# Softmax over 512 columns: the first store issued ahead of two exponentials of the second tile

## Chip, cores, metric

One core of one Trainium2 chip. The metric is the device time of one execution in microseconds (us). Before: 162.81 us, the median of three runs (162.79 to 162.98).

## The reference

```python
# x: (16, 1024, 512) float32
x_scaled = x / 0.5
x_max = np.max(x_scaled, axis=-1, keepdims=True)
exp_x = np.exp(x_scaled - x_max)
return (exp_x / np.sum(exp_x, axis=-1, keepdims=True)).astype(np.float32)
```

33.55 MB are read and 33.55 MB written.

## The kernel before

The 16384 rows are eight tiles of 128 partitions by 16 rows of 512 floats, 4.19 MB each. There are six buffers, so the seventh tile needs the buffer of the first, and its load waits for the first tile's store. VectorE takes the maxima, the reciprocals and most of the final multiplication; ScalarE takes the exponentials (one per row, with the sum) and one row in eight of the multiplication, and issues the stores.

```python
G = 16
LOADS = [[(0, 4), (4, G)]] + [WHOLE] * 7
BLOCKS = [[(0, 4), (4, 8), (8, G)]] + [WHOLE] * 6 + [[(0, 8), (8, G)]]
STORES = [WHOLE] * 8
SPLIT, TAIL = 6, 2          # seventh tile: its last two rows come by GpSimd
BUFS = 6
# ... cut
if c == SPLIT and hi == G:
    hi = G - TAIL
    for p0, p1 in ((P - 2, P), (0, P - 2)):
        nc.gpsimd.dma_start(out=xt[p0:p1, hi:G, :], in_=xr[c][p0:p1, hi:G, :], max_dma_last_dim=4 * D)
nc.sync.dma_start(out=xt[:, lo:hi, :], in_=xr[c][:, lo:hi, :])
# ... cut: shift (maxima, VectorE), exponentials (ScalarE)
def scale_vector(i):
    k = b - b // 8          # the rows that VectorE multiplies
    # ... cut: reciprocal, tensor_mul of k rows
def scale_scalar(i):
    for g in range(b - b // 8, b):      # the others, on ScalarE
        # ... cut
# ... cut
shift(0)
shift(1)
exponentials(0)
for i in range(n):          # n = 11 blocks; the first tile is blocks 0 to 2
    if i + 1 < n:
        exponentials(i + 1)
    scale_vector(i)
    scale_scalar(i)
    if i + 2 < n:
        shift(i + 2)
    store(i)                # issues on ScalarE's queue when a tile is complete
```

Of the kernel before, what the change touches and what calls it, by code (L numbers as in the profile page):

```python
# [1 line left out]

# [4 lines left out]


@with_exitstack
def kernel(  # L10
    ctx: ExitStack,
    tc: tile.TileContext,
    x: bass.AP,
    out: bass.AP,
):
    nc = tc.nc
    fp32 = mybir.dt.float32
    P = nc.NUM_PARTITIONS
    AX = mybir.AxisListType.X
    EXP = mybir.ActivationFunctionType.Exp  # L20
    COPY = mybir.ActivationFunctionType.Copy
    MAX = mybir.AluOpType.max

    D = x.shape[-1]
    xf = x.flatten_outer_dims()
    of = out.flatten_outer_dims()
    N = xf.shape[0]




    G = 16
    C = N // (P * G)
    assert C * P * G == N
    xr = xf.rearrange("(c p g) d -> c p g d", p=P, g=G)
    outr = of.rearrange("(c p g) d -> c p g d", p=P, g=G)
    WHOLE = [(0, G)]
# [3 lines that stand above are left out]
    SPLIT, TAIL = 6, 2  # L41
    BMAX = 16
    BUFS = 6

    data = ctx.enter_context(tc.tile_pool(name="data", bufs=BUFS))
    stats = ctx.enter_context(tc.tile_pool(name="stats", bufs=6))

    ctx.enter_context(tc.manual_schedule())


    warm = stats.tile([P, 1], fp32, name="warm", bufs=1)
    nc.vector.memset(warm, 0.0)  # L52
    nc.scalar.activation(out=warm, in_=warm, func=EXP)  # L53

    chunks = {}
    blocks = [(c, lo, hi) for c in range(C) for lo, hi in BLOCKS[c]]
    n = len(blocks)
    biases, sums, recips = {}, {}, {}

    def load(c):  # L60
        if c < BUFS:
            chunks[c] = data.tile([P, G, D], fp32, name="xt")
        else:
            chunks[c] = chunks[c - BUFS]
        xt = chunks[c]
        for lo, hi in LOADS[c]:
# [7 lines that stand above are left out]
                    nc.gpsimd.dma_start(  # L74
                        out=xt[p0:p1, hi:G, :],
                        in_=xr[c][p0:p1, hi:G, :],
                        max_dma_last_dim=4 * D,
                    )
            nc.sync.dma_start(out=xt[:, lo:hi, :], in_=xr[c][:, lo:hi, :])  # L79

    def shift(i):
        c, lo, hi = blocks[i]
        if c not in chunks:
            load(c)
        b = hi - lo
        negmax = stats.tile([P, BMAX], fp32, name="negmax")
        nc.vector.tensor_reduce(  # L87
            negmax[:, 0:b], chunks[c][:, lo:hi, :], axis=AX, op=MAX, negate=True
        )
        biases[i] = stats.tile([P, BMAX], fp32, name="bias")  # L90
        nc.vector.tensor_scalar_mul(biases[i][:, 0:b], negmax[:, 0:b], 2.0)  # L91

    def exponentials(i):
        c, lo, hi = blocks[i]
        sums[i] = stats.tile([P, BMAX], fp32, name="sums")
        for g in range(hi - lo):
            row = chunks[c][:, lo + g, :]
            nc.scalar.activation(  # L98
                out=row,
                in_=row,  # L100
                func=EXP,
                bias=biases[i][:, g : g + 1],
                scale=2.0,
                accum_out=sums[i][:, g : g + 1],
            )


    def scale_vector(i):
        c, lo, hi = blocks[i]
        b = hi - lo  # L110
        k = b - b // 8
        recips[i] = stats.tile([P, BMAX], fp32, name="recip")
        nc.vector.reciprocal(recips[i][:, 0:b], sums[i][:, 0:b])  # L113
        rows = chunks[c][:, lo : lo + k, :]
        nc.vector.tensor_mul(  # L115
            rows, rows, recips[i][:, 0:k].unsqueeze(2).broadcast_to((P, k, D))
        )

    def scale_scalar(i):
        c, lo, hi = blocks[i]  # L120
        b = hi - lo
        for g in range(b - b // 8, b):
            row = chunks[c][:, lo + g, :]
            nc.scalar.activation(  # L124
                out=row, in_=row, func=COPY, scale=recips[i][:, g : g + 1]
            )

    def store(i):
        c, _, end = blocks[i]
        for lo, hi in STORES[c]:  # L130
            if hi == end:
                nc.scalar.dma_start(
                    out=outr[c][:, lo:hi, :], in_=chunks[c][:, lo:hi, :]
                )

    shift(0)
    shift(1)
    exponentials(0)
    for i in range(n):
        if i + 1 < n:  # L140
            exponentials(i + 1)
        scale_vector(i)
        scale_scalar(i)
        if i + 2 < n:
            shift(i + 2)
        store(i)


# [1 line left out]
_INS = ['x']  # L150
_OUTS = [((16, 1024, 512), 'float32')]


# [23 lines left out]
```

## Time and profile before

| what | before |
|---|---|
| time | 162.81 us |
| span of the profiled run | 160.9 us |
| VectorE busy, ScalarE busy | 134.6 us (84%), 102.1 us (63%) |
| moved | 67.13 MB, 417 GB/s over the span |
| first store | issued 45.61, landed 71.05 us |
| seventh tile's rows by GpSimd | issued 72.52, landed 103.57 us |
| last store | issued 147.58, landed 159.89 us |

A share of busy time does not tell what sets the end. Here VectorE and DMA both look full. Two lines of the kernel before, the last store's issue (timeline: start, duration, engine, line, operation) and GpSimd's larger piece (list of DMA issues: count, size, us from issue to landing):

```profile
147.58 0.34 ACTq L132 DMA_DIRECT2D out_dram<-xt  x1
```

```profile
xt<-in_x_dram POOLq DMA_DIRECT2D x1, 504.0 KB, 31.1
```

### The profile page before, as it was taken

To read this page: it belongs to the slowest core of one execution; us is meant where nothing else is said; L and a number is where in the kernel's file an instruction comes from. 1 tells how busy PE (TensorE), PEld (TensorE's weight loads), DVE (VectorE), ACT (ScalarE), POOL (GpSimd) and SP (SyncE) were. 2 spreads that over 40 slices of the span, in tenths; PEclk is the share of its full clock that TensorE was granted. 3 is DMA by queue.
4 is the path that set the end of the run, shared out by engine and by line. 5 is a ranking of instruction groups with operands and counts; after the bars stand their busy time and mean duration, and the time that the engine had idled before them with its cause. 6 is when DMAs were issued, how large, how long until landed. Compare 5 with 4: busy or idle time off the path is not lost.

```text
span 160.9 us, 410 instructions
## 1 busy us (share of the span) xinstructions
DVE 134.6 (84%) x45; ACT 102.1 (63%) x273; POOL 1.7 (1%) x6
## 2 busy tenths in 40 slices
DVE  0507999999999999999999999999999999956000
ACT  3071549069979963997299909990999890890000
POOL 0000000000000000012000000000000000000000
DMA  5999999999999999999999999999999999999993
GB/s 175 476 399 505 399 391 513 399 391 507 399 399 375 407 456 440 407 440 441 424 444 417 397 447 462 440 399 464 432 399 464 440 399 456 448 399 440 456 399 138
DMA packets 2642, 67.13 MB, mean 417 GB/s; under 512 B 336, under 2 KB 336, under 8 KB 464
## 3 DMA queue, kind: packets, MB, share of 16 engines
q1 hardware_dynamic: 1296, 33.03, 48.5%
q10 hardware_dynamic: 1152, 33.55, 48.3%
q0 software_dynamic: 192, 0.52, 0.8%
q14 instruction: 2, 0.02, 0.0%
HBM read 33.55 MB, written 33.55 MB: 417 GB/s over the span
## 4 chain that ended last, share of the span: by engine, by line
DVE 79%; DMA 7%; ACT 4%; issue 1%; SPq 0%
DVE negmax L87 42%; DVE xt L115 36%; DMA xt<-in_x_dram 7%; ACT xt L98 4%; DVE bias L91 1%; DVE recip L113 1%; SPq L79 0%
## 5 line engine op out<-in xcount | busy, mean ns | idle before, releaser
L98 ACT ACTIVATE xt<-xt,bias 128x512 f32<-128x512 f32 x128 | 90.4, 708 | 41.7 <-DVE bias L91 41.2
L87 DVE TENSOR_REDUCE negmax<-xt 128x16 f32<-128x8192 f32 (+2 forms) x11 | 69.9, 6352 | 9.5 <-DMA xt<-in_x_dram 9.5
L115 DVE TENSOR_TENSOR xt<-xt,recip 128x7168 f32<-128x7168 f32 (+2 forms) x11 | 62.0, 5637 | 0.4
L98 ACT ACTIVATION_READ_ACCUMULATOR xt<-xt,bias 128x1 f32 x128 | 23.9, 187 | 0.0
L124 ACT ACTIVATE xt<-xt,recip 128x512 f32<-128x512 f32 x15 | 9.9, 707 | 0.0
L113 DVE RECIPROCAL recip<-sums 128x16 f32<-128x16 f32 (+2 forms) x11 | 2.4, 219 | 1.8 <-ACT xt L98 1.8
L91 DVE TENSOR_SCALAR bias<-negmax 128x16 f32<-128x16 f32 (+2 forms) x11 | 1.9, 173 | 0.4
L74 POOL DMA_DIRECT2D xt<-in_x_dram x2 | 1.5, 736 | 71.4 <-DMA out_dram<-xt 71.4
L53 ACT ACT_TABLE_LOAD x1 | 1.3, 1283 | 0.7 <-PEq L161 0.7
L52 DVE MEMSET warm<- 128x1 f32 x1 | 0.1, 59 | 0.8 <-PEq L161 0.8
L53 ACT ACTIVATE warm<-warm 128x1 f32<-128x1 f32 x1 | 0.2, 202 | 0.0
L161 POOL MEMSET const-float32-0.0<- 128x1 f32 x1 | 0.1, 93 | 0.2 <-issue 0.2
L161 POOL MEMSET const-bfloat16-1.0<- 128x1 bf16 x1 | 0.1, 95 | 0.0
L161 POOL MEMSET const-float32-1.0<- 128x1 f32 x1 | 0.1, 93 | 0.0
L161 POOL MEMSET const-uint8-127<- 128x1 uint8 x1 | 0.1, 93 | 0.0
## 6 DMA issues: line engine op xcount, KB each, us to landing
out_dram<-xt ACTq DMA_DIRECT2D x8, 4096.0 KB, 23.7
xt<-in_x_dram SPq DMA_DIRECT2D x6, 4096.0 KB, 35.0
xt<-in_x_dram SPq DMA_DIRECT2D x1, 3584.0 KB, 23.8
xt<-in_x_dram SPq DMA_DIRECT2D x1, 3072.0 KB, 11.7
xt<-in_x_dram SPq DMA_DIRECT2D x1, 1024.0 KB, 4.9
xt<-in_x_dram POOLq DMA_DIRECT2D x1, 504.0 KB, 31.1
xt<-in_x_dram POOLq DMA_DIRECT2D x1, 8.0 KB, 9.3
```

The lines of the kernel that those rows point to most:

```text
L52: nc.vector.memset(warm, 0.0)
L53: nc.scalar.activation(out=warm, in_=warm, func=EXP)
L74: nc.gpsimd.dma_start(out=xt[p0:p1, hi:G, :], in_=xr[c][p0:p1, hi:G, :], max_dma_last_dim=4 * D,)
L87: nc.vector.tensor_reduce(negmax[:, 0:b], chunks[c][:, lo:hi, :], axis=AX, op=MAX, negate=True)
L91: nc.vector.tensor_scalar_mul(biases[i][:, 0:b], negmax[:, 0:b], 2.0)
L98: nc.scalar.activation(out=row, in_=row, func=EXP, bias=biases[i][:, g : g + 1], scale=2.0, accum_out=sums[i][:, g : g + 1],)
L113: nc.vector.reciprocal(recips[i][:, 0:b], sums[i][:, 0:b])
L115: nc.vector.tensor_mul(rows, rows, recips[i][:, 0:k].unsqueeze(2).broadcast_to((P, k, D)))
L124: nc.scalar.activation(out=row, in_=row, func=COPY, scale=recips[i][:, g : g + 1])
L161: nc = _bacc.Bacc("TRN2", target_bir_lowering=False, num_devices=1)
```

## The change

Its intent: the first store is the one whose landing lets the seventh tile load, so it goes out before the last two exponentials of the second tile. The loads, GpSimd's two pieces included, are left as they were.

```diff
-    def exponentials(i):
+    def exponentials(i, rows):
         c, lo, hi = blocks[i]
-        sums[i] = stats.tile([P, BMAX], fp32, name="sums")
-        for g in range(hi - lo):
+        if i not in sums:
+            sums[i] = stats.tile([P, BMAX], fp32, name="sums")
+        for g in rows:
...
-    exponentials(0)
+
+    def rows(i):
+        c, lo, hi = blocks[i]
+        cut = hi - lo - (2 if c == 1 else 0)
+        return range(cut), range(cut, hi - lo)
+
+    exponentials(0, rows(0)[0])
     for i in range(n):
         if i + 1 < n:
-            exponentials(i + 1)
+            exponentials(i + 1, rows(i + 1)[0])
         scale_vector(i)
         scale_scalar(i)
         if i + 2 < n:
             shift(i + 2)
         store(i)
+        if i + 1 < n:
+            exponentials(i + 1, rows(i + 1)[1])
```

## The prediction

> **What bounds the kernel now.** I began with the page of the profile: the slices, then the queues and the issues.
>
> ```profile
> DVE  0507999999999999999999999999999999956000
> ACT  3071549069979963997299909990999890890000
> DMA  5999999999999999999999999999999999999993
> GB/s 175 476 399 505 399 391 513 399 391 507 399 399 375 407 456 440 407 440 441 424 444 417 397 447 462 440 399 464 432 399 464 440 399 456 448 399 440 456 399 138
> HBM read 33.55 MB, written 33.55 MB: 417 GB/s over the span
> out_dram<-xt ACTq DMA_DIRECT2D x8, 4096.0 KB, 23.7
> ```
>
> Two rows are full: VectorE from slice 5 to slice 36, and the DMA from slice 2 to the last but one. So two claims have to be weighed: a chain through VectorE, and the mass of bytes. The chain of waits names VectorE:
>
> ```profile
> DVE 79%; DMA 7%; ACT 4%; issue 1%; SPq 0%
> ...
> 87.42 8.61 DVE negmax L87
> ...
> 96.42 7.19 DVE xt L115
> 103.61 0.35 issue
> 103.96 8.69 DVE negmax L87
> ...
> 137.59 5.76 ACT xt L98 x16
> 143.35 0.02 issue
> 143.37 0.21 DVE recip L113
> 143.59 0.02 issue
> 143.61 3.89 DVE xt L115
> ```
>
> From 12.90 us on this chain has no hole. The 0.35 us "issue" at 103.61 looks like a wait for the seventh tile's load, but the instruction before it, the multiplication that starts at 96.42, takes 7.62 us by the timeline and ends at 104.04; the reduction starts while it drains, as the others do. So VectorE does not wait there, and an earlier load cannot pull it forward. The chain ends in the issue of the last store (timeline, ACT's queue): start 147.58. That store lands at 159.89, and the span ends at 160.9.
>
> Those last 12.3 us are DMA. I went through the records of the single DMA packets in the trace, summed by time. From 2 us to 158 us the packets in flight fill 16.0 of 16 engines in every 2 us, with one dip to 15.8 at 146 to 150 us. A 32 KB packet takes 1.21 us, load or store, and one engine does 8 of them for a whole tile: 9.7 us. The store of the seventh tile ends on 14 of the engines between 148.77 and 149.56 us, on one at 147.52 and on one at 149.87. The early engine begins its part of the last store at about 148.4, some 0.85 us after the issue at 147.58. Thus 14 engines pass from one store to the next without a gap, with only about 148.77 - 148.4 = 0.35 us in hand. **The DMA engines are the bound, from the first load to the last store, and the VectorE chain runs just ahead of them.** The finish is set by the slowest of 16 engines: the final store's completions come at 158.17 to 158.92 on 14 engines, 159.25 on one, 159.55 on the last. The mean over all packets ends near 158.7, so imbalance costs about 0.8 us.
>
> **What the Trainium skill says.** "DMA: Bandwidth & Descriptors", section "Issuing engines are not separate DMA queues": transfers issued from ACT, SyncE and GpSimd run on the same 16 engines and interleave. The trace agrees: when stores join the loads, from 50 us to 112 us, the two queues take about 8 engines each, and the total stays at 16.0. The same page, section "Queues, rings and completion order": each engine alternates between its queues packet by packet. The trace agrees: GpSimd's 504 KB, 4 KB packets of 0.16 us, issue at 72.52 and land only at 103.57, since each of about 9 packets per engine waits its turn behind a 32 KB load packet and a 32 KB store packet. Section "Why a DMA increments its semaphore by 16 and not by 1" says how many engines a transfer uses, and that GpSimd's transfers take consecutive engines from a cursor. Chaining the packets end to start, I find two engines that carry two or three 4 KB packets and 14 that carry seven to ten (the chaining is not perfect: one and nine would fit the shape), so the split into 2 and 126 rows relieves two engines of 8 x 0.16 = 1.3 us. "Perfetto Trace Analysis", section "What "DMA-bound" means", names specific DMA engines as one possible bound; the 159.55 against a median of 158.6 is that case.
>
> **The change, part by part.** Nothing is removed or added: 128 exponentials, 15 scaling rows, 8 stores, the same loads by the same queues, the same VectorE program. One order changes, on ACT, and only in tile two (the condition names it).
>
> ```profile
> 42.76 0.70 ACT L98 ACTIVATE xt<-xt,bias 128x512 f32<-128x512 f32 x1
> ...
> 43.46 0.70 ACT L98 ACTIVATE xt<-xt,bias 128x512 f32<-128x512 f32 x1
> ...
> 44.17 0.70 ACT L98 ACTIVATE xt<-xt,bias 128x512 f32<-128x512 f32 x1
> ...
> 44.87 0.70 ACT L124 ACTIVATE xt<-xt,recip 128x512 f32<-128x512 f32 x1
> 45.61 0.38 ACTq L132 DMA_DIRECT2D out_dram<-xt  x1
> 46.20 0.17 DVE L91 TENSOR_SCALAR bias<-negmax 128x16 f32<-128x16 f32 x1
> 46.28 0.24 DVE L113 RECIPROCAL recip<-sums 128x16 f32<-128x16 f32 x1
> ```
>
> The rows at 43.46 and 44.17 are the fifteenth and sixteenth exponentials of tile two. They move behind the store. The scaling row then starts at 43.46 in place of 44.87, and the store issues at 45.61 - 1.41 = 44.20. Its VectorE input has been ready since 37.6, so nothing else holds it. First gain: **the first store starts 1.4 us sooner**.
>
> What ACT pays: the issue itself. After the issue at 125.53, the next exponential starts at 125.97, so it takes about 0.47 us from the scaling row's end. Before, that stood in an idle gap (ACT waits for a bias until 46.41). After, the two exponentials run at about 44.65 to 46.05, and the read of their sum, which trails by about 0.1 us, ends near 46.15. VectorE's reciprocal needs these sums at 46.28. So it fits, with some 0.1 us in hand; if not, VectorE's chain slips by perhaps 0.1 us, and so does the last store's issue, inside the 0.35 us above.
>
> Downstream: the first store lands at about 69.7 instead of 71.05, which releases the buffer for the seventh tile. SyncE's 14-row load and GpSimd's two pieces go out 1.4 us sooner, and GpSimd's rows land near 102.2 instead of 103.57. Since VectorE gets to them at 103.96 either way, this is margin and not time. The loads of tiles five and six lose a share of DMA in exchange (they landed at 56.43 and 75.80, and are needed at 70.7 and 87.3), harmless.
>
> The sum for the DMA bound: the same 67.1 MB in the same packets on engines that were never idle gives 0. Moving work between the queues of a full resource does not shorten it.
>
> What can move is the imbalance. When the first store joins, about 30 load packets between 47.1 and 50 us take 1.3 to 2.85 us rather than 1.21; the excess sums to some 15 engine-us, 0.9 us per engine. One engine, already about 0.5 us late since an instruction-fetch packet at 37.8, takes the 2.85 us packet: it completes tile five at 56.10 against a median of 54.3, 1.8 us late, and I take it to be the one that finishes last at 159.55, 0.95 us late, after being relieved. An earlier start of the store changes the phase of this event, thus how much the laggard loses. If it loses no more than the others, the end is set by the 159.25 or 158.92 engine: gain 0.3 to 0.6 us. If it loses one more packet's time, the loss is up to 1.2 us. The 2.85 us is the largest of all those packets, so a return towards the usual is likelier than a further rise: I take -0.2 us as my estimate, 162.81 - 0.2 = **162.6 us**.
>
> **The rivals.** (1) The VectorE chain is the true bound and the earlier load shortens it: the 0.35 us at 103.61 would go, 162.45. Against: the multiplication ends at 104.04, so there was no wait. Even then the effect is tiny. (2) The late exponentials hold the reciprocal, and a wait on ACT takes the place of the one removed: up to 0.5 us of slip through a chain without slack, minus the 0.35 us in hand, 162.8 to 163.0. For it: the slack is only 0.1 us. (3) The first store's disturbance meets the loads in a worse phase, and one engine ends later: 163 to 164. For it: one engine did take 1.6 us in one packet. (4) The disturbance vanishes: up to 0.9 us of DMA time saved, but the last store cannot move data before 148.4, so at best 148.4 + 9.7 = 158.1 in place of 159.55: 161.4, which is 0.9%. This is also the floor for every version with this VectorE chain.
>
> **Range and chances.** The floor of 161.4 and a bad phase of one packet (1.2 us, 164.0) bracket what I can imagine; both ends are unlikely. 8 in 10: 162.0 to 163.4. The three times of before span 0.2 us, so noise is small. A 2% step is 3.3 us, more than twice any term above: faster 0.01, within 2% 0.97, slower 0.02.
>
> **What would show it.** Right: the store's issue at about 44.2 in ACT's queue; its landing near 69.7, GpSimd's pieces landing near 102; VectorE's reductions still 16.6 us apart and the last store's issue within 0.15 us of 147.58; DMA slices at 9 throughout. The completions of the last store by engine would tell whether the laggard moved. Wrong: a last store issued over 0.3 us earlier or later (the VectorE chain was moved), a hole in the DMA row, or an end beyond 164 with the issue unmoved, which would mean that one engine fell behind for a reason I have not seen.

## The result, and the profile after

After: 162.66 us, median of four runs (162.54 to 162.85), beside 162.80 us for the kernel before on the same chip. The ratio is 0.9994, 95% interval 0.9976 to 1.0012: the same. (A ratio is the mean time of one kernel's fast runs over that of the other's fast runs of the same rounds, so not quite the ratio of the medians.)

The timeline of the changed kernel where the change is (ScalarE's instructions, and two of VectorE's):

```profile
42.71 0.70 ACT L99 ACTIVATE xt<-xt,bias 128x512 f32<-128x512 f32 x1
...
43.41 0.71 ACT L125 ACTIVATE xt<-xt,recip 128x512 f32<-128x512 f32 x1
44.15 0.38 ACTq L133 DMA_DIRECT2D out_dram<-xt  x1
44.57 0.72 ACT L99 ACTIVATE xt<-xt,bias 128x512 f32<-128x512 f32 x1 [0.45 <-ACT xt L125]
...
45.29 0.71 ACT L99 ACTIVATE xt<-xt,bias 128x512 f32<-128x512 f32 x1
45.90 0.19 ACT L99 ACTIVATION_READ_ACCUMULATOR xt<-xt,bias 128x1 f32 x1
46.15 0.17 DVE L91 TENSOR_SCALAR bias<-negmax 128x16 f32<-128x16 f32 x1
46.24 0.24 DVE L114 RECIPROCAL recip<-sums 128x16 f32<-128x16 f32 x1
```

The store issues at 44.15 in place of 45.61. The two late exponentials start 0.45 us after the scaling row's end (the bracket is ScalarE's idle time), the last sum is read by 46.09, and the reciprocal takes it at 46.24 without a wait.

The same slices, the chain of waits around the seventh tile, the last store, and GpSimd's piece, all of the changed kernel:

```profile
DVE  0607999999999999999999999999999999956000
ACT  3071549069989963998299909990999890790000
POOL 0000000000000000030000000000000000000000
DMA  5999999999999999999999998999999999999993
```

```profile
96.37 2.91 DVE xt L116
99.28 4.64 issue
103.92 8.69 DVE negmax L87
```

```profile
147.53 0.34 ACTq L133 DMA_DIRECT2D out_dram<-xt  x1
```

```profile
xt<-in_x_dram POOLq DMA_DIRECT2D x1, 504.0 KB, 29.6
```

Look at the second of these fences and at its counterpart in the prediction. "4.64 issue" is not a wait that has grown from 0.35 us. The chain steps at 99.28 to the moment at which the load released the reduction, while VectorE was still multiplying until 104.0; both reductions start within 0.04 us of the same time (103.96 and 103.92). So the piece called "issue" is the margin of the load: 0.35 us before, 4.64 us after. The change multiplied this margin, and nothing in this kernel spends it. It is not free: the eighth tile's load landed 0.9 us later than before (115.61, before 114.72), though VectorE reads it only at 120.5. The last store issues at 147.53, 0.05 us from before.

So the time neither went nor came: the first store's issue moved by 1.46 us, its landing by 2.84, GpSimd's rows by 4.33, and the end by about 0.1 us.

To see why, I read the records of the single DMA packets in the trace. A packet of 32 KB takes 1.213 us when nothing disturbs it (28 KB: 1.062, 24 KB: 0.91). "Excess" below is what packets took over that, summed over all that were more than 0.03 us too long, and divided by 16 engines. "Mean end" and "last end" are the mean and the last of the 16 engines' completions of the last store. All times in us, from the one profiled execution of each kernel; the rows below the first two are the experiments.

| kernel | first store issued | last store issued | excess per engine | mean end | last end | time of that run |
|---|---|---|---|---|---|---|
| before | 45.61 | 147.58 | 1.01 | 158.71 | 159.55 | 162.72 |
| after | 44.15 | 147.53 | 1.29 | 159.01 | 159.31 | 162.61 |
| after, again | 44.15 | 147.53 | 1.23 | 158.88 | 159.26 | 162.58 |
| pieces swapped | 44.22 | 147.60 | 1.07 | 158.76 | 159.30 | 162.48 |
| light VectorE | 43.68 | 141.24 | 1.05 | 158.67 | 159.37 | 162.63 |
| before, light VectorE | 44.93 | 141.19 | 1.26 | 158.79 | 159.24 | 162.51 |
| five behind | 41.84 | 147.96 | 1.29 | 158.90 | 159.21 | 162.52 |
| eight behind | 39.76 | 147.72 | 1.68 | 159.25 | 160.26 | 163.44 |
| eight behind, light | 39.49 | 145.86 | 2.18 | 159.79 | 160.70 | 163.95 |
| twelve behind | 37.48 | 148.62 | 1.85 | 159.53 | 159.83 | 163.11 |
| store in halves | 24.82 | 148.23 | 1.40 | 159.12 | 159.58 | 162.82 |
| halves, light | 28.07 | 148.45 | 1.80 | 159.47 | 161.65 | 165.02 |
| store late | 47.88 | 149.68 | 2.01 | 160.35 | 160.67 | 163.87 |
| half a store left out | 44.06 | 147.43 | 1.24 | 158.08 | 158.18 | 161.37 |

Take the excess from the mean end: in the first twelve rows 157.5 to 157.7 remains (the last two, with 158.3 and 156.8, are special: in both, engines stood idle), whether the first store goes out at 25 or at 45 us, and whether the last goes out at 141 or at 149 us. That is the time of 67.13 MB through engines that are never idle. From the last end to the time of the run it is another 3.2 to 3.4 us, always. These twelve can differ from each other only in two small terms: the excess, and how far the last engine lags the mean. This is an account of where the time is, not yet of why. The change moved both, in opposite directions: excess 1.01 to 1.29 (+0.28), lag 159.55 - 158.71 = 0.84 to 159.31 - 159.01 = 0.30 (-0.54). The sum is -0.26 us; the last end moved by -0.24 us and that run's time by -0.11 us, within what runs of one kernel differ by.

The same records, split by time, say where the excess is. From 1 us before to 9 us after the issue of the first store, when this store joins the loads, it is 0.7 to 1.2 us per engine in every version: 0.93 before, 0.87 after. What comes later, most of it between 60 and 110 us, is 0.06 us before and 0.40 after, and 0.1 to 1.3 us in the other versions. So the excess of the changed kernel did not rise at the joining but later; there, 5.9 of 6.4 us (summed over the engines) are in the 28 KB packets of the seventh tile's load. Why these ran slower is not shown.

### The profile page after: what moved, and what is told of

It reads as the page before. It is cut to its first block, busy times and chain, and to the rows that moved or that the text cites. A ratio compares the mean times of both kernels' runs of the same rounds, so it can differ in the third digit from the quotient of the medians.

```text
span 160.8 us, 410 instructions
## 1 busy us (share of the span) xinstructions
DVE 134.6 (84%) x45; ACT 102.2 (64%) x273; POOL 1.7 (1%) x6
## 2 busy tenths in 40 slices
DMA packets 2642, 67.13 MB, mean 417 GB/s; under 512 B 336, under 2 KB 336, under 8 KB 464
## 4 chain that ended last, share of the span: by engine, by line
DVE 77%; DMA 7%; ACT 4%; issue 3%; SPq 0%
DVE negmax L87 42%; DVE xt L116 33%; DMA xt<-in_x_dram 7%; ACT xt L99 4%; DVE bias L91 1%; DVE recip L114 1%; SPq L79 0%
## 6 DMA issues: line engine op xcount, KB each, us to landing
xt<-in_x_dram POOLq DMA_DIRECT2D x1, 504.0 KB, 29.6
```

## The experiments

Twelve kernels ran. Experiments 5, 9, 10 and 12 ran on chip 4, the others on chip 1, and each ratio is to the kernel before on the same chip. The runs of the kernel before spread from 162.33 to 163.50 us, wider than the three first runs had suggested.

**1. The changed kernel again, unaltered.**

> The changed kernel once more, unaltered, with more rounds, since its first interval (0.9976 to 1.0012) spans more than the difference. Theory (nothing is gained): ratio 0.998 to 1.002. Rival (my own 0.2 us from a luckier slowest engine): 0.9988 or below with an interval that excludes 1.

Measured: 162.66 us (162.55 to 162.96), ratio 0.9991, interval 0.9969 to 1.0013. The same. My 0.2 us can neither be confirmed nor refused at this width; a gain of 1% is out.

**2. A lighter VectorE chain**, to ask which of the two full rows is the bound.

```diff
-        k = b - b // 8
+        k = b - b // 4
-        for g in range(b - b // 8, b):
+        for g in range(b - b // 4, b):
```

> The changed kernel with four rows of sixteen scaled on ScalarE in place of two, which takes some 1.07 us of VectorE from each whole tile, about 8 us in all. Theory (DMA is the bound, the VectorE chain runs just ahead of it): the last store issues several us before 147.5, but the time stays between 162.2 and 162.7. Rival (the chain through VectorE, 77% of the chain of waits, is the bound): 155 to 159.

Measured: 162.57 us, ratio 0.9986, interval 0.9965 to 1.0008. The last store (timeline) issues 6.3 us sooner:

```profile
141.24 0.34 ACTq L133 DMA_DIRECT2D out_dram<-xt  x1
```

It lands at 159.81, where it landed at 159.78 in the changed kernel. 77% of the chain of waits is VectorE, and 6 us of it are worth nothing: the bytes are the bound.

**3. Less to move**: the first half of the fourth tile is not stored, so the result is wrong.

```diff
-    STORES = [WHOLE] * 8
+    STORES = [WHOLE] * 3 + [[(0, 0), (8, G)]] + [WHOLE] * 4
```

> The changed kernel without the store of the first half of tile four (its result is wrong on purpose): 2.1 MB less, 4.9 us less for each DMA engine. Theory (DMA bound, with the VectorE chain 0.35 us behind it, so the floor of 161.4 applies): the last store still issues at 147.5, every engine begins it near 148.4 and ends near 158.1, DMA shows a hole before it, and the time is 161.2 to 161.5. If only DMA counted: 157.8. If only the VectorE chain counted: 162.66, unchanged.

Measured: 161.42 us (161.37 to 161.48), ratio 0.991, interval 0.9887 to 0.9933. 4.9 us less for every engine give only 1.2 us (against the 162.66 of the changed kernel). In the stretches around the last store's issue (columns: stretch, its length, busy us of VectorE, ScalarE, GpSimd, granted clock, DMA share, GB/s), first the changed kernel:

```profile
146.00:148.40 2.40, 1.45 (x1) 0.00 (x0) 0.00 (x0) 1.00 0.98 423
148.40:158.00 9.60, 0.00 (x0) 0.00 (x0) 0.00 (x0) 1.00 0.98 423
```

and then this one:

```profile
146.00:148.40 2.40, 1.36 (x1) 0.00 (x0) 0.00 (x0) 1.00 0.44 191
148.40:158.00 9.60, 0.00 (x0) 0.00 (x0) 0.00 (x0) 1.00 0.91 389
```

The hole ahead of 148.4 shows the floor: here DMA waits for the VectorE chain. All 16 engines end between 158.02 and 158.18. So there are two bounds, some 1.2 us apart, and to take away more than that both have to go.

**4. The first store later**, from the kernel before: after eight exponentials of the next block in program order. (The part of the diff in which `exponentials` gets its first and last row is cut.)

```diff
-        if i + 1 < n:
-            exponentials(i + 1)
+        if i == 3:
+            exponentials(4, 0, 8)
+            store(2)
+            exponentials(4, 8)
+        elif i + 1 < n:
+            exponentials(i + 1)
...
-        store(i)
+        if i != 2:
+            store(i)
```

> The kernel before with its first store issued later, after eight exponentials of tile three, near 52 us. Theory (DMA conserves work: the queued loads of tiles five and six fill the engines until about 60 us anyway): the store lands at 71 to 73, GpSimd's rows land at 103 to 106, VectorE waits at most 2 us for them, and the time is 162.3 to 163.4; if mixing loads and stores costs time, it is at the low end of that. Rival (each us of delay of this store is paid in full): 168 to 169.

Measured: 163.72 us (163.48 to 164.60), ratio 1.0058, interval 1.0033 to 1.0083. A part of the expectation missed: the store issued at 47.88, not near 52, while the third of the eight exponentials ahead of it was running. By this trace, a DMA whose inputs are ready is issued when ScalarE's sequencer comes to it, not when the instructions before it have run. So the store is only 2.3 us later than before. That is enough to use up the margin. The timeline of VectorE at the seventh tile:

```profile
96.34 7.63 DVE L116 TENSOR_TENSOR xt<-xt,recip 128x7168 f32<-128x7168 f32 x1
106.07 8.69 DVE L87 TENSOR_REDUCE negmax<-xt 128x16 f32<-128x8192 f32 x1 [2.10 <-DMA xt<-in_x_dram]
```

VectorE waits 2.10 us for GpSimd's rows (landed at 105.99), the last store issues 2.10 us later than before, at 149.68, and 149.68 + 0.85 (issue to first packet, as in the prediction) + 9.7 us of data = 160.2, which is where the engines end (mean 160.35). All 16 engines end within 0.4 us of each other, and from 148 to 152 us they stood idle for 0.7 us each: they waited for this store. Of the 2.1 us, 0.9 show in the time; the rest was the lead that the VectorE chain has on the DMA. Not all of the 0.9 need be the wait's: the excess of this run also rose, by 1.0 us, and by that alone the mean end would be near 157.6 + 2.0 = 159.6 (an estimate). Here is what the margin is for: the kernel before is 0.35 us from this stall, the changed one 4.6 us.

**5. The margin with a lighter VectorE chain**: the edit of experiment 2 on the kernel before.

> The kernel before with four rows of sixteen scaled on ScalarE. VectorE reaches the seventh tile near 98.5, GpSimd's rows land near 103.6, so it waits about 5 us where the changed kernel with the same lighter chain waited 1 us. Theory (DMA is the bound and the margin is no time): still 162.3 to 162.9, last store issued before 147. Rival (the margin is time once VectorE is faster): above 163.2.

Measured: 162.78 us, ratio 1.0006, interval 0.9994 to 1.0019. The expected time, but not by the expected wait: in this kernel the store issued at 44.93 and GpSimd's rows landed at 99.80, so VectorE waited 1.9 us and not 5. The rival is not supported, but the test was weaker than planned.

**6. GpSimd's pieces in the other order**, to see if the last engine of all is one of those that the short piece relieves.

```diff
-                for p0, p1 in ((P - 2, P), (0, P - 2)):
+                for p0, p1 in ((0, P - 2), (P - 2, P)):
```

> The changed kernel with GpSimd's two pieces issued in the other order, 126 rows first. If the slowest DMA engine is one of the two that the short piece relieves, the relief now goes to two other engines: the slow one carries 8 more packets of 0.16 us, ends 1.1 to 1.3 us later than the 159.3 of the changed kernel, and the time is 163.6 to 164.0. Rival (which engine is slow is chance, or the relief goes to other engines than the slow one): 162.4 to 162.9, unchanged.

Measured: 162.85 us (162.48 to 163.50), ratio 1.0008, interval 0.9984 to 1.0032. The loss of 1 us did not come; by this interval, which engines are relieved is worth 0.3% at most. My reading of the slowest engine falls with this. Chaining the packets of each engine (one starts as the one before ends, to some ns) shows that the edit did what it should: 14 engines carry nine of GpSimd's 4 KB packets and two carry one. Before and after, one of these two is the engine that also carries both instruction fetches; it ends at 158.64 and 158.71, and another engine is the last. With the pieces swapped two other engines are relieved and end first (158.32 and 158.35), and the fetching engine ends last of all, at 159.31. So the relief counts for the engine that gets it, and not for the time, because another engine ends as late without it.

**7. Eight exponentials behind the store, in place of two.**

```diff
-        cut = hi - lo - (2 if c == 1 else 0)
+        cut = hi - lo - (8 if c == 1 else 0)
```

> The changed kernel with eight exponentials of tile two behind the first store in place of two. Theory (the 16 DMA engines are full from first load to last store, so when a store joins does not matter): the store issues near 40.0 us, 4.2 us earlier than in the changed kernel, the last store still issues at 147.5 to 147.7, and the time is 162.4 to 162.9, same as both kernels. Rival (each us that the first store starts earlier is worth something): the time falls below 162.2.

Measured: 163.62 us (163.34 to 164.11), ratio 1.0048, interval 1.0026 to 1.0071. Neither: the store went out at 39.76 as expected, and the kernel lost 0.8 us. "When a store joins does not matter" is not quite true. The eighth tile's load landed at 120.70 (114.72 before), with stores taking a share of the DMA for longer ahead of it, and VectorE waited 0.3 us for it. The last completion came 1.0 us after the mean of the engines, and the excess rose to 1.68 us: 1.03 at the joining (0.93 before) and 0.65 later (0.06).

**8. Eight behind, with the lighter VectorE chain**, to separate these two causes.

> Eight exponentials behind the first store, and four rows of sixteen scaled on ScalarE. The kernel with eight behind took 0.8 us more than before; in its profile VectorE also waited 0.2 us for the eighth tile's load, which landed at 120.7 in place of 114.7. If that wait is the cause, the lighter VectorE chain (last store issued 5 us sooner) takes the loss away: 162.3 to 162.8. If the cause is in the DMA itself (its packets took 27 engine-us more than at full speed, against 16 before), the loss stays: 163.2 to 163.9.

Measured: 163.93 us (163.20 to 164.17), ratio 1.0057, interval 1.0033 to 1.0080. The last store issued at 145.86, not 5 but two us sooner than with eight behind alone, since the faster VectorE now waited 5.6 us for the loads of the last two tiles. From there 145.86 + 0.85 + 9.7 = 156.4, long before the engines end, so this wait is not what sets the time; yet the loss stayed. It is in the DMA: excess 2.18 us per engine (0.89 at the joining, 1.29 later), and a group of four engines that ends 0.8 to 0.9 us after the mean.

**9. and 10. Five and twelve behind** (the same edit with 5 and with 12).

> The changed kernel with five exponentials behind the first store (issue near 41.9 us, between the 44.2 of two behind and the 39.8 of eight behind). If the loss of eight behind grows with the lead of the store: about 163.1 to 163.3. If it depends on how the store's start falls against the packets and loads then under way: anything from 162.5 to 164, in no order.

> Twelve exponentials behind the first store: it waits for VectorE's multiplication, which ends near 37.5, so the issue is near 37.7 us. If the loss grows with the lead: 164 or more. If it depends on how the start falls: anything from 162.5 to 164. In both cases the eighth tile's load lands near 121, and VectorE waits some tenths of a us for it.

Measured: five 162.52 us (162.43 to 163.57), ratio 1.0008, interval 0.9987 to 1.0030; twelve 163.09 us (162.71 to 163.36), ratio 1.0025, interval 1.0010 to 1.0039. With two, five, eight and twelve behind, the ratio is 0.999, 1.001, 1.005 and 1.003: no steady growth with the lead, though the intervals of eight overlap those of five and twelve, which ran on another chip, so an order among the three is not shown. The loss follows the excess and the lag of each arrangement. I had thought of the way in which the store's start falls among the packets under way. The split by time leaves this a small part at most: at the joining the excess is 0.94, 1.03 and 1.17 us with five, eight and twelve behind (0.93 before), later 0.35, 0.65 and 0.68 (0.06 before). Most of what was added came 12 us and more after the joining; its cause stays open.

**11. The first tile's store in halves**, the first one 19 us earlier.

```diff
-    STORES = [WHOLE] * 8
+    STORES = [[(0, 8), (8, G)]] + [WHOLE] * 7
```

> The changed kernel with the first tile's store cut in two: rows 0 to 7 go out as soon as they are scaled, near 25 us, the rest where it was. If the slow packets of 46 to 49 us belong to the moment in which the first store joins the loads, they move to 28 to 31 us. If they belong to that time or to ScalarE's queue, they stay. Time: if the DMA only conserves work, 162.4 to 162.9; if a longer stretch in which loads and stores are mixed costs time, as the run with eight behind suggests, 163.3 to 164.5.

Measured: 162.63 us (162.46 to 163.16), ratio 0.9987, interval 0.9963 to 1.0010. The slow packets moved. Here are the same stretches of the changed kernel and of this one (columns as in experiment 3):

```profile
24.00:28.00 4.00, 4.00 (x2) 4.00 (x12) 0.00 (x0) 1.00 1.04 451
28.00:32.00 4.00, 4.00 (x1) 0.07 (x1) 0.00 (x0) 1.00 1.08 467
32.00:36.00 4.00, 3.93 (x4) 2.47 (x7) 0.00 (x0) 1.00 0.91 393
...
44.00:48.00 4.00, 3.93 (x4) 3.28 (x10) 0.00 (x0) 1.00 0.98 344
```

```profile
24.00:28.00 4.00, 4.00 (x2) 4.00 (x12) 0.00 (x0) 1.00 1.19 475
28.00:32.00 4.00, 4.00 (x1) 0.11 (x2) 0.00 (x0) 1.00 0.94 360
32.00:36.00 4.00, 3.93 (x4) 2.43 (x7) 0.00 (x0) 1.00 0.85 344
...
44.00:48.00 4.00, 3.93 (x4) 3.28 (x10) 0.00 (x0) 1.00 0.91 393
```

(Bytes are counted where packets begin or end, so a single stretch can be off by some per cent.) In the changed kernel 344 GB/s stand at 44 to 48 us; here 360 and 344 at 28 to 36 us. The packet records say it without that blur: packets of 1.3 to 1.8 us between 26.4 and 32.5 us, and only one at 1.46 us between 33 and 80. So the slow packets belong to the first store's joining the loads. And this kernel mixes stores with loads for longer than any of experiments 7 to 10 (from 26 to 121 us), without a loss: a long mixed stretch alone is not what costs time.

**12. Halves, with the lighter VectorE chain**, as the best that I could put together.

> The first store in halves together with the lighter VectorE chain, as the best version that these runs suggest. With the chain out of the way only DMA is left: 162.2 to 162.7, perhaps a little under both kernels, not by 1%. If the early half stalls the loads for the faster VectorE: 163 or more.

Measured: 163.27 us (162.81 to 165.59), ratio 1.0051, interval 1.0013 to 1.0089. Above the expected range, and unsteady. In the profiled run, at 165.02, VectorE waited 8.1 us for the loads of the last two tiles, and one engine completed at 161.65, 2.2 us after the mean. No version beat both kernels clear of noise. The nearest, the lighter VectorE chain, has an interval that contains 1.

## Why the prediction was right

**The bound.** Right, and shown: DMA has no hole worth the name (the prediction counted one dip to 15.8 engines, and the records have a second of the same size at 48 to 50 us), 6 us less VectorE chain change nothing (experiment 2), and the sum "157.6 plus excess" holds through the first twelve rows of the table. Moving work between the queues of the same full engines was worth 0.

**The floor.** Right in mechanism and size: 161.4 as worked out, 161.42 measured with half a store left out.

**The store's issue and ScalarE's price.** 44.20 predicted, 44.15 measured; last sum predicted near 46.15, measured 46.09; the reciprocal did not wait. Rival 2 falls.

**What follows the store.** The direction was right, the sizes too small: first store landed at 68.21 (predicted 69.7), GpSimd's rows at 99.24 (102.2). I carried the 1.4 us through one to one. But a landing is that of the slowest of 16 engines: before, the last engine finished this store at 70.75 and the median one at 68.80; after, 67.85 and 67.66. The median moved by 1.1 us, and the straggler vanished: that is the other 1.8 us of the last engine's 2.9. GpSimd's rows then also had a shorter way from issue to landing, 29.6 us in place of 31.1. (The prediction's account of the 31.1 is short: nine packets that each wait for two of 1.21 us make some 23 us. The trace has twelve packets of GpSimd's queue on each engine, some of 4 or 8 bytes only, and the first of them starts at 76.0, 3.5 us after the issue.) SyncE's 14 rows of the seventh tile did not come sooner at all (95.55, before 94.94): they stand in one queue behind the sixth tile's load, which landed at 77.22 in place of 75.80 because the store took its share earlier. None of it reached the end.

**The imbalance.** The term of -0.2 us was in the right order, but it is smaller than the noise, and a step of its working failed, so that 162.6 came so near to 162.66 is in part luck. The step: "One engine, already about 0.5 us late since an instruction-fetch packet at 37.8, takes the 2.85 us packet". Chaining the packets of each engine again, with the order of its queues as a constraint, gives two engines. The one with the fetch completed tile five last (56.10), but the first store first (68.20): it had only switched to the store sooner and was not late in total. The one with the 2.85 us packet completed tile five first (53.81), the first store last (70.75), and the whole last of all, at 159.55. In the changed kernel the engine with the fetch packets again completes tile five last (57.18) and the store first (66.86), and ends early, at 158.71. (The chaining leaves a few packets unplaced.) So the lateness of one load tells nothing about an engine that serves two queues, and the last engine is not one that GpSimd's short piece relieves (experiment 6). What I expected of the straggler came, 159.55 to 159.31; what I did not expect was that the excess of all engines would rise by 0.28 us and take half of it back, and not at the joining, where I looked for it, but after 60 us. Rival 4, that the disturbance vanishes, did not come: 0.93 us per engine at the joining before, 0.87 after.

**The noise.** "The three times of before span 0.2 us, so noise is small" was wrong: in 11 runs together, the same kernel spread over 1.1 us.

**What stays open.** Why first packets beside a new store run slow; why packets run slow again between 60 and 110 us, by amounts that differ between versions; and with this, why eight behind costs 0.8 us. Rival 3, a worse phase at the joining, did not come true for this change, and it accounts for little of experiments 7 to 10, where most of the added excess came later.

## What to carry to other kernels

When the DMA row is full from the first load to the last store, look first at the bytes: here the order of the transfers was worth nothing except through slow packets and how evenly the 16 engines end, 0.6% at most. Count bytes before moving instructions. A "wait" or "issue" on the chain next to a load's landing can be margin rather than time: compare when the engine before it really ended. And margin has a use: the kernel before was 0.35 us from a stall, and a store 2.3 us later cost it 0.9 us, while the changed kernel has 4.6 us (that it would bear such a delay was not run).

## What the Trainium skill lacked or had wrong

- "DMA: Bandwidth & Descriptors", section "Where 436 GB/s comes from", says that for transfers between HBM and SBUF the HBM side, some 358 GB/s for a core, binds. Read alone, this misleads: here one core moved 417 GB/s over its whole span, loads and stores together. The page's own table, 425 GB/s for the loads of one core, is the one that fits, and the note under it keeps the lower figure for two cores that stream at once; the section says "binds" without that condition.
- The same page, section "Queues, rings and completion order", has the engines alternate between queues, with no cost for it. When the first store joined the loads, some 30 packets took 1.3 to 2.85 us in place of 1.21, 0.9 us per engine, and this moved with the store to 26 to 32 us (experiment 11). Between 60 and 110 us the packets of a mixed stretch lost another 0.06 to 1.3 us per engine.
- "Runtime: NRT & Kernel Launch", section "Instruction fetch mechanics", calls the cost of a fetch mostly hidden. In a kernel with full DMA it is not quite: two packets of 0.31 us (at 37.8 and 97.5 us) beside load packets of 1.59 and 1.55 us, some 0.7 us each with what they delay, on the engine that they fall on.
- "Perfetto Trace Analysis", section "Sequencer Loop", says that instructions are pushed into a queue ahead of the engine, but not that the issue of a DMA can so overtake instructions that stand before it (the depth of the queue is on another page): in experiment 4 a store with eight exponentials ahead of it in program order was issued while the third was running.
